# Four tiles of a SwiGLU layer from seven block products back to eight

## The chip, the cores and the metric

The kernel runs on one core of a Trainium2 chip. The metric is the device time of one execution in microseconds (us), from the first instruction to the last with the little that lies around them. The engines that matter here are TensorE (PE, matrix products), VectorE (DVE, element-wise work on two operands), ScalarE (ACT, element-wise functions and copies) and the DMA queue of SyncE (SP), which fetches all weights.

## What is computed

A decoder trunk of two layers over 512 tokens of width 1024, in float32. Each layer is an attention mixer, then a SwiGLU feed-forward block, each behind a norm whose scale and shift come from a vector `c`:

```
for l in range(2):
    sh1, sc1, g1, sh2, sc2, g2 = split(silu(c) @ ada_w[l] + ada_b[l], 6)
    h = rms_norm(x, norm_mix[l]) * (1 + sc1) + sh1
    y = mixer(h)                       # layer 0: two kinds of attention; layer 1: windowed
    x = x + g1 * (y @ w_out[l])
    h = rms_norm(x, norm_ffn[l]) * (1 + sc2) + sh2
    x = x + g2 * ((silu(h @ ffn_gate[l]) * (h @ ffn_up[l])) @ ffn_down[l])
```

The change lies in `h @ ffn_gate[0]` and `h @ ffn_up[0]`: 512 tokens by 1024 by 2816, twice.

## The kernel before

**Precision.** Every float32 product is made of three: an operand is split into a high part `hi` (rounded) and a low part `lo` (what is left), and `mm3` (L441) issues hi·hi, hi·lo and lo·hi into one accumulator. The split of an operand costs a copy on ACT (hi) and a subtraction on DVE (lo).

**Feed-forward block.** The 2816 hidden features are 22 tiles of 128, in two parts of 11 (`FPARTS`; tiles 0 to 10, then 11 to 21). After each part `reduce_out` (L1124) multiplies its hidden tiles by the down weights. A tile needs a 1024 by 128 block of the gate weights and one of the up weights, one DMA of 1 MB (`raw`), and its products are made in one of two ways:

- `ffn_tile` (L1153), eight block products: for each of 8 blocks of the inner dimension, gate and up, one `mm3` over all 512 tokens. That is 8 x 2 x 3 = 48 matmuls of 512 columns. The weights are split by `split_w` (L571): four subtractions of 128x512 on DVE. Two instructions of DVE take the result.
- `ffn_seven` (L1190), seven block products in place of eight, of the kind that Strassen's and Winograd's schemes use: the products run over half of the tokens (256 columns), 7 x 4 x 3 = 84 matmuls, on sums of weight blocks. `prep_seven` (L579) makes these sums and splits them: on DVE three instructions of 128x1024 and five of 128x512 per tile. Six instructions of DVE combine the products and split the hidden tile. The sums on the token side are made once per layer by `combos` (L1167): 24 instructions on DVE.

Before, tiles 0 to 2 of both layers went through `ffn_tile`, all others through `ffn_seven` (L569, L1240). Two of the first tiles are done in two halves of the tokens, since the norm ends by halves.

**Background work.** In layer 0's feed-forward block the modulation vectors that come later (the last of layer 0 and all six of layer 1) are computed in between by `mod_rest` (L693) as weighted sums on DVE: one step of two instructions on 128x512 after each tile (`NBG[0] = 1`), four steps after each output tile of `reduce_out`. Layer 1 has none of it. Its DMAs share the three `raw` buffers with the weights.

**Buffers.** Prepared weights lie in a pool `w` of 13 buffers of 128x1024: a tile in eight products holds 4, one in seven holds 7 and an eighth for a while. Accumulators (`ps`) are 8 banks.

**Order.** Operations are recorded first and put in order by `Sched` (L163 on): a list scheduler walks through them with the planner's own durations, gives DVE's operations due times worked back from PE's order, does this in up to eight rounds and keeps the round that it thinks shortest. So the place of each instruction on each engine is fixed when the kernel is built, buffers are handed out in that order, and each engine runs its own list strictly in order. A different list of operations in one place can change the order everywhere.

Of the kernel before, what the change touches and what calls it, by code (L numbers as in the profile page):

```python
# [25 lines left out]
BIG = 1e30  # L26
NW, NT2 = 13, 59

SEVEN, DIRECT = (0, 1), 3
NBG = (1, 4)  # L30
TOPK = 128
LAM_INIT = 0.2
# [340 lines left out]
class Kern:  # L373
# [192 lines left out]

    def seven(self, i):
        name, idx, _ = self.units[i]
        return name[:2] == "wg" and int(name[2]) in SEVEN and idx >= DIRECT  # L569

    def split_w(self, i, src, n, step, e="DVE"):  # L571
        hi, lo = (self.s.tile("w", "w", (P, 1024), FR)[:, :n] for _ in range(2))
# [194 lines left out]

    def norm_tile(self, l, n, k, c, r, H):
        sh = self.mod[l][:, 3 * n, k:k + 1]
        if n == 1 and l in SEVEN:  # L770
            if c.start == 0:
                if k == 0:
                    self.hf = []
                self.hf.append(self.t2("T"))
            t = self.hf[k][:, c]
        else:
            t = self.t2("nt")[:, c]
        hi, lo = H[k][0][:, c], H[k][1][:, c]
        self.stt(t, self.x[k][:, c], self.G[l][n][:, k:k + 1], r, OP.mult, OP.mult)
        self.act(hi, t, AF.Identity, bias=sh)  # L780
        self.stt(lo, t, sh, hi.bitcast(F), OP.add, OP.subtract)
# [443 lines left out]
    def ffn(self, l, H, last):  # L1225
        T = None
        for pi, (a, b) in enumerate(FPARTS):
            hid = [(self.t2("hid", dt=FR), self.t2("hid", dt=FR)) for _ in range(a, b)]
            W = {}

            def w(f):
                if f not in W:
                    W[f] = self.unit()
                return W[f]
            jobs = []
            if pi == 0:
                jobs = [(a + e, c) for c in HALVES for e in range(2)]
            jobs += [(f, ALL) for f in range(a + len(jobs) // 2, b)]
            for f, c in jobs:
                if l not in SEVEN or f < DIRECT:  # L1240
                    sg = self.ffn_tile(H, f, c, w(f), hid[f - a])
                else:
                    T = T or self.combos(l)
                    sg = self.ffn_seven(H, T, w(f), hid[f - a])
                self.lnexp = []
                if l == 0 and f == FT - 1:
                    self.act_table([sg])
                self.run_bg(NBG[0])
            self.reduce_out(l, hid, 5, pi == 1, last if pi == 1 else lambda m, c: None)
# [125 lines left out]
```

## Time and profile before

| | |
|---|---|
| time, median of 3 runs | 1195.58 us (1195.43 to 1197.99) |
| the profiled execution: its own time | 1197.88 us |
| the profiled execution: its span | 1196.1 us, granted TensorE clock 0.993 |
| busy: PE, DVE, ACT, POOL | 97%, 77%, 51%, 7% |
| layer 0's feed-forward block | about 301 to 674 us of the span |
| layer 1's feed-forward block | about 843 to 1196 us |

The page's busy share of PE is high all along, so the rows to look at are those that show where PE stands still, and what it waits for there. Matmuls overlap in the trace (one of 256 columns is recorded as 283 ns while a new one starts every 120 ns), so rates are read from counts over long windows and not from the mean of one.

### The profile page before, as it was taken

The page shows a single profiled execution, that of the slowest core. Times are in us where ns is not written, and L with a number is a line of the kernel's source. Part 1 is how long each engine was busy: PE and PEld are TensorE (multiplying, and loading weights), DVE is VectorE, ACT ScalarE, POOL GpSimd, SP SyncE. Part 2 cuts the span into 40 slices and gives each one's busy share as a digit, 9 for nine tenths or more (in the row PEclk, how much of TensorE's full clock was granted, in tenths as well). Part 3 has the DMA queues.
Part 4 walks back from the last instruction along what each step waited for, and adds up shares of the span by engine and source line. Part 5 has one row for each costly group of instructions (what it writes and reads, how often), then busy time and mean ns, then how long its engine had stood idle before and what let it go on. Part 6 is the DMA issues. An engine that isn't in the chain of part 4 may idle for free.

```text
span 1196.1 us, 20044 instructions
## 1 busy us (share of the span) xinstructions
PE 1163.8 (97%) x7792; PEld 1003.9 (84%) x7792; DVE 924.7 (77%) x2008; ACT 613.0 (51%) x1416; POOL 83.1 (7%) x224
## 2 busy tenths in 40 slices
PE   6989899999989999999999999999999999999998
PEld 3867677679989988999889976668999988999988
DVE  5589999856998978899984867755999844688831
ACT  5554266864754531354642657774766532566510
POOL 0132332300000000000000021100000000000000
PEclk9999999999998999999999999999999999999999
DMA  9635614012233377745372121012123342123411
GB/s 349 246 128 176 224 59 141 36 37 71 71 141 141 110 290 282 245 148 193 126 263 108 71 106 72 1 36 107 62 81 106 113 152 71 71 107 106 151 44 37
DMA packets 32432, 151.81 MB, mean 127 GB/s; under 512 B 3152, under 2 KB 4304, under 8 KB 21072
## 3 DMA queue, kind: packets, MB, share of 16 engines
q1 hardware_dynamic: 32336, 150.52, 35.3%
q8 instruction: 61, 1.00, 0.3%
q14 instruction: 35, 0.29, 0.1%
HBM read 148.41 MB, written 2.10 MB: 126 GB/s over the span
## 4 chain that ended last, share of the span: by engine, by line
PE 83%; DVE 8%; ACT 1%; issue 0%; DVEq 0%
PE ps L434 79%; PE ps L445 4%; DVE w L476 2%; DVE t L491 1%; DVE t L911 1%; DVE sm L910 1%; DVE t L476 1%; ACT t L460 1%; DVE raw L476 0%; DVE t L496 0%; ACT w L460 0%; DVE sm L502 0%; DVE t L484 0%; DVE x L491 0%; DVE ps L476 0%
## 5 line engine op out<-in xcount | busy, mean ns | idle before, releaser
L434 PE MATMUL ps<-t,w 128*128 128x256 f32 (+2 forms) x5664 | 822.9, 306 | 10.6 <-ACT t L460 5.7
L434 PEld LDWEIGHTS ps<-t,w 128*128 128x128 f32 x5664 | 759.6, 192 | 64.5 <-ACT t L460 9.2
L460 ACT ACTIVATE w<-raw 128x512 fp32r<-128x512 f32 (+1 forms) x364 | 227.7, 668 | 154.3 <-PE ps L434 98.8
L476 DVE TENSOR_TENSOR w<-raw,w 128x512 fp32r<-128x512 f32 (+1 forms) x340 | 249.7, 762 | 56.2 <-PE ps L434 42.7
L460 ACT ACTIVATE t<-ps 128x256 f32<-128x256 f32 (+6 forms) x388 | 154.6, 426 | 198.5 <-PE ps L434 131.7
L434 PE MATMUL ps<-w,t 128*128 128x512 f32 (+1 forms) x768 | 191.4, 391 | 0.8 <-DVE t L491 0.8
L434 PEld LDWEIGHTS ps<-w,t 128*128 128x128 f32 x768 | 133.1, 190 | 35.1 <-issue 8.2
L476 DVE TENSOR_TENSOR t<-t,t 128x256 f32<-128x256 f32 (+3 forms) x163 | 83.5, 536 | 15.8 <-ACT t L460 15.8
L476 DVE TENSOR_TENSOR t<-ps,t 128x256 f32<-128x256 f32 (+4 forms) x196 | 76.5, 410 | 20.1 <-ACT t L460 10.3
L491 DVE SCALAR_TENSOR_TENSOR x<-ps,mod,x 128x512 f32<-128x512 f32 (+1 forms) x64 | 39.3, 615 | 65.8 <-PE ps L434 65.6
L434 PE MATMUL ps<-t,t 64*128 64x256 f32 (+5 forms) x592 | 87.9, 357 | 0.7 <-ACT t L460 0.4
L434 PEld LDWEIGHTS ps<-t,t 64*128 64x128 f32 (+2 forms) x592 | 56.5, 186 | 32.9 <-issue 19.5
L491 DVE SCALAR_TENSOR_TENSOR t<-raw,cond,t 128x512 f32<-128x512 f32 x112 | 77.8, 746 | 1.4 <-DMA raw<-in_ada 1.4
L460 ACT ACTIVATE t<-t 128x512 fp32r<-128x512 f32 (+3 forms) x109 | 55.0, 522 | 32.5 <-DVE t L476 31.9
L460 ACT ACTIVATE t<-t,sm 128x256 f32<-128x256 f32 (+3 forms) x128 | 65.5, 515 | 11.9 <-DVE sm L496 11.1
L445 PE MATMUL ps<-cst,t 128*128 128x128 f32 x388 | 61.1, 278 | 8.9 <-DVE t L476 7.3
L445 PEld LDWEIGHTS ps<-cst,t 128*128 128x128 f32 x388 | 45.0, 140 | 29.4 <-DVE t L476 7.0
L460 ACT ACTIVATE w<-w 128x1024 fp32r<-128x1024 f32 x38 | 40.2, 1058 | 43.9 <-PE ps L434 41.5
L496 DVE CUSTOM_DVE_ANT_0 t<-ps,cst 128x256 f32<-128x256 f32 (+3 forms) x104 | 39.3, 409 | 26.1 <-PE ps L434 26.0
L476 DVE TENSOR_TENSOR w<-w 128x1024 fp32r<-128x1024 f32 x38 | 46.4, 1222 | 10.7 <-PE ps L434 10.4
L484 POOL TENSOR_SCALAR sm<-sm 128x8 f32<-128x8 f32 (+2 forms) x64 | 16.4, 256 | 514.6 <-DVE sm L502 502.3
L460 ACT ACTIVATE t<-t,mod 128x256 fp32r<-128x256 f32 (+2 forms) x72 | 37.8, 572 | 24.1 <-DVE t L491 24.0
(74 smaller groups left out, 620.4 us busy)
## 6 DMA issues: line engine op xcount, KB each, us to landing
raw<-in_wg SPq DMA_DIRECT2D x44, 1024.0 KB, 4.8
raw<-in_ada SPq DMA_DIRECT2D x40, 1024.0 KB, 5.3
raw<-in_wd SPq DMA_DIRECT2D x20, 1024.0 KB, 4.8
raw<-in_w0c SPq DMA_DIRECT2D x10, 1024.0 KB, 6.3
t<-in_ada SPq DMA_DIRECT2D x32, 256.0 KB, 6.6
raw<-in_wo SPq DMA_DIRECT2D x8, 1024.0 KB, 4.8
raw<-in_w1c SPq DMA_DIRECT2D x6, 1024.0 KB, 4.9
x<-in_x SPq DMA_DIRECT2D x8, 256.0 KB, 4.4
```

What stands on the lines that cost most here:

```text
L434: self.nc.tensor.matmul(o.ap(), l.ap(), r.ap(), start=st, stop=sp, skip_group_check=True)
L445: self.s.op("PE", 107, lambda: self.nc.tensor.transpose(out.ap(), src.ap(), self.ident.ap()), [out], [src, self.ident])
L460: self.nc.scalar.activation(out.ap(), src.ap(), func, **kw)
L476: lambda: self.eng(e).tensor_tensor(out.ap(), a.ap(), b.ap(), op=op), [out], [a, b])
L484: self.eng(e).tensor_scalar(out.ap(), a.ap(), val(s1), val(s2), op0=op0, **kw)
L491: lambda: self.eng(e).scalar_tensor_tensor(out.ap(), a.ap(), val(s), b.ap(), op0=op0, op1=op1),
L496: lambda: self.nc.vector.tensor_tensor_reduce(out.ap(), a.ap(), b.ap(), op0=OP.add, op1=OP.min, scale=scale, scalar=3e38, accum_out=accum. ...
L910: self.s.op("DVE", 65 + 1.05 * n, lambda m8=m8: self.nc.vector.max(m8.ap(), sc.ap()), [m8], [sc])
L911: self.s.op("DVE", 65 + 1.05 * n, lambda m8=m8: self.nc.vector.match_replace(sc.ap(), m8.ap(), sc.ap(), -3e38), [sc], [m8, sc])
```

## The change

Four tiles of layer 0 go back from `ffn_seven` to `ffn_tile`: tiles 4 and 6 (the fifth and seventh of the first part) and tiles 11 and 13 (the first and third of the second). `EIGHT` lists by layer which tiles use eight block products. Layer 1 keeps 0, 1 and 2. The line of `norm_tile` says the same as before, since both layers were in `SEVEN`.

```diff
-SEVEN, DIRECT = (0, 1), 3
+EIGHT = ((0, 1, 2, 4, 6, 11, 13), (0, 1, 2))
@@ def seven(self, i)
-        return name[:2] == "wg" and int(name[2]) in SEVEN and idx >= DIRECT
+        return name[:2] == "wg" and idx not in EIGHT[int(name[2])]
@@ def norm_tile(self, l, n, k, c, r, H)
-        if n == 1 and l in SEVEN:
+        if n == 1:
@@ def ffn(self, l, H, last)
-                if l not in SEVEN or f < DIRECT:
+                if f in EIGHT[l]:
                     sg = self.ffn_tile(H, f, c, w(f), hid[f - a])
```

The order is worked out anew. On PE it is the same up to the middle of layer 0's mixer and differs in places from there on; DVE's differs from a little earlier. Three places on DVE, the engine that prepares the weights.

DVE where tile 4's weights are prepared, from the first instruction of the modulation on (`t<-raw,cond`). `w<-raw,w` and `w<-w` are pieces of a tile's preparation, `<-ps` takes a product. Before:

```order
L484 TENSOR_SCALAR t_4149<-raw,cond 128x512
L484 TENSOR_SCALAR t_4159<-raw,cond 128x512
L491 SCALAR_TENSOR_TENSOR t_4149<-raw,cond,t_4149 128x512
L491 SCALAR_TENSOR_TENSOR t_4159<-raw,cond,t_4159 128x512
L476 TENSOR_TENSOR w<-w 128x1024
L476 TENSOR_TENSOR w<-raw,w 128x512 x2
L476 TENSOR_TENSOR t_4154<-ps,t_4133 128x256
L476 TENSOR_TENSOR w<-raw,w 128x512
```

Now:

```order
L476 TENSOR_TENSOR w<-raw,w 128x512 x6
L484 TENSOR_SCALAR t_4139<-raw,cond 128x512
L476 TENSOR_TENSOR ps<-ps,t_4122 128x256
L484 TENSOR_SCALAR t_4148<-raw,cond 128x512
L491 SCALAR_TENSOR_TENSOR t_4139<-raw,cond,t_4139 128x512
L491 SCALAR_TENSOR_TENSOR t_4148<-raw,cond,t_4148 128x512
```

Before, four of tile 4's pieces stood behind the modulation's first four instructions; now all four of its pieces (the last four of the `x6`; the first two are tile 3's) stand ahead of them.

DVE where tile 5's weights are prepared. Before:

```order
L476 TENSOR_TENSOR w<-raw 128x1024
L476 TENSOR_TENSOR w<-raw,w 128x1024
L476 TENSOR_TENSOR raw<-w,raw 128x512
L476 TENSOR_TENSOR w<-w 128x1024
L476 TENSOR_TENSOR w<-raw,w 128x512
L476 TENSOR_TENSOR raw<-raw 128x512
L476 TENSOR_TENSOR ps<-ps,t_4238 128x256
L491 SCALAR_TENSOR_TENSOR t_4149<-raw,cond,t_4149 128x512
L491 SCALAR_TENSOR_TENSOR t_4159<-raw,cond,t_4159 128x512
L476 TENSOR_TENSOR w<-raw 128x1024
L476 TENSOR_TENSOR w<-raw,w 128x512
L476 TENSOR_TENSOR raw<-w,raw 128x512
```

Now:

```order
L476 TENSOR_TENSOR w<-raw 128x1024
L476 TENSOR_TENSOR w<-raw,w 128x1024
L476 TENSOR_TENSOR raw<-w,raw 128x512
L476 TENSOR_TENSOR w<-w 128x1024
L476 TENSOR_TENSOR w<-raw,w 128x512
L476 TENSOR_TENSOR raw<-raw 128x512
L491 SCALAR_TENSOR_TENSOR t_4139<-raw,cond,t_4139 128x512
L491 SCALAR_TENSOR_TENSOR t_4148<-raw,cond,t_4148 128x512
L476 TENSOR_TENSOR w<-raw,w 128x512
L491 SCALAR_TENSOR_TENSOR t_4139<-raw,cond,t_4139 128x512
L491 SCALAR_TENSOR_TENSOR t_4148<-raw,cond,t_4148 128x512
L476 TENSOR_TENSOR w<-raw,w 128x512
```

Before, tile 6's preparation (the second `w<-raw 128x1024`) began ahead of the last pieces of tile 5; now tile 5 is finished with nothing of tile 6 ahead of it.

DVE at the end of the preparation of tile 17, in the second part. Before:

```order
L476 TENSOR_TENSOR w<-raw,w 128x1024
L476 TENSOR_TENSOR raw<-w,raw 128x512
L476 TENSOR_TENSOR t_6335<-ps,t_6285 128x256
L476 TENSOR_TENSOR raw<-raw 128x512
L476 TENSOR_TENSOR w<-w 128x1024
L491 SCALAR_TENSOR_TENSOR t_6062<-raw,cond,t_6062 128x512
L476 TENSOR_TENSOR w<-raw,w 128x512 x2
L491 SCALAR_TENSOR_TENSOR t_6069<-raw,cond,t_6069 128x512
L476 TENSOR_TENSOR ps<-ps,t_6425 128x256
L491 SCALAR_TENSOR_TENSOR t_6062<-raw,cond,t_6062 128x512
L491 SCALAR_TENSOR_TENSOR t_6069<-raw,cond,t_6069 128x512
L476 TENSOR_TENSOR w<-raw,w 128x512 x2
```

Now:

```order
L476 TENSOR_TENSOR w<-raw,w 128x1024
L476 TENSOR_TENSOR w<-raw 128x1024
L476 TENSOR_TENSOR w<-raw,w 128x512
L476 TENSOR_TENSOR ps<-ps,t_6122 128x256
L476 TENSOR_TENSOR raw<-w,raw 128x512
L476 TENSOR_TENSOR w<-raw,w 128x512
L476 TENSOR_TENSOR raw<-raw 128x512
L476 TENSOR_TENSOR t_6071<-ps,t_6041 128x256
L476 TENSOR_TENSOR w<-raw 128x1024
L491 SCALAR_TENSOR_TENSOR t_5786<-raw,cond,t_5786 128x512
L476 TENSOR_TENSOR t_6149<-ps,t_6122 128x256
L476 TENSOR_TENSOR w<-w 128x1024
```

Before, the last piece of tile 17 (the first of the closing `x2`) stood behind seven of the eight pieces of tile 18 and four modulation instructions; now two pieces of tile 18 and one modulation instruction stand among those of tile 17, and its last two pieces follow right behind the rows shown.

## Rows read from the trace of the kernel before

**Rows 1.** The page's part 2: busy tenths in 40 slices.
```profile
PE   6989899999989999999999999999999999999998
DVE  5589999856998978899984867755999844688831
```

**Rows 2.** Windows: stretch, length; PE, PEld, DVE, ACT, POOL busy; PEclk; DMA.
```profile
346.00:368.00 22.00, 17.26 (x112) 16.09 (x112) 19.38 (x33) 11.40 (x22) 0.00 (x0) 0.84 0.53 194
549.00:585.00 36.00, 31.66 (x254) 29.74 (x253) 35.77 (x60) 20.04 (x39) 0.00 (x0) 1.00 0.43 157
```

**Rows 3.** Timeline of PE, 346 to 368 us; in brackets idle time before, releaser.
```profile
345.81 1.48 PE L434 MATMUL ps<-t,w 128*128 128x256 f32 x11
347.77 4.69 PE L434 MATMUL ps<-t,w 128*128 128x256 f32 x36 [0.47 <-ACT t L460]
352.93 1.69 PE L434 MATMUL ps<-t,w 128*128 128x256 f32 x12 [0.47 <-ACT t L460]
355.64 1.69 PE L434 MATMUL ps<-t,w 128*128 128x256 f32 x12 [1.02 <-ACT t L460]
359.38 2.07 PE L434 MATMUL ps<-t,w 128*128 128x256 f32 x12 [2.04 <-DVE t L476]
362.18 5.99 PE L434 MATMUL ps<-t,w 128*128 128x256 f32 x29 [0.73 <-DVE t L476]
```

**Rows 4.** Timeline of PE, 549 to 585 us.
```profile
551.63 6.02 PE L434 MATMUL ps<-t,w 128*128 128x256 f32 x48 [1.01 <-ACT t L460]
558.12 3.13 PE L434 MATMUL ps<-t,w 128*128 128x256 f32 x24 [0.47 <-ACT t L460]
561.90 7.46 PE L434 MATMUL ps<-t,w 128*128 128x256 f32 x60 [0.66 <-DVE t L476]
570.78 4.58 PE L434 MATMUL ps<-t,w 128*128 128x256 f32 x36 [1.42 <-ACT t L460]
...
579.50 3.13 PE L434 MATMUL ps<-t,w 128*128 128x256 f32 x24 [0.31 <-DVE t L476]
583.11 1.69 PE L434 MATMUL ps<-t,w 128*128 128x256 f32 x12 [0.47 <-ACT t L460]
```

**Rows 5.** Chain of waits in 346 to 368 us, then 549 to 585: shares.
```profile
by line: PE ps L434 32.7%; DVE w L476 27.2%; ACT w L460 11.5%; DVE t L491 9.9%; DVE raw L476 7.6%; issue 3.4%; DVE t L476 3.1%; ACT t L460 3.0%; DVE ps L476 2.0%
...
by line: PE ps L434 34.2%; DVE w L476 32.7%; DVE t L491 13.3%; DVE raw L476 8.4%; issue 5.7%; DVE t L476 3.1%; ACT t L460 1.1%; DVE ps L476 0.9%; PE ps L445 0.6%; DVEq L476 0.1%
```

**Rows 6.** Windows: the clock behind the longest wait.
```profile
362.00:366.00 4.00, 3.83 (x18) 3.83 (x19) 3.38 (x10) 2.41 (x8) 0.00 (x0) 0.50 0.96 380
```

**Rows 7.** Windows in layer 1: tiles in seven products, then down products.
```profile
885.00:945.00 60.00, 60.00 (x502) 60.00 (x501) 54.57 (x90) 38.63 (x73) 0.00 (x0) 1.00 0.31 107
970.00:1015.00 45.00, 45.00 (x200) 37.26 (x199) 18.02 (x24) 9.83 (x14) 0.00 (x0) 1.00 0.27 94
```

**Rows 8.** Groups by form on DVE: count, busy us, mean ns, idle before.
```profile
L476 DVE TENSOR_TENSOR w<-raw,w 128x512 fp32r<-128x512 f32 x300 | 203.1, 706 | 43.4 <-PE ps L434 30.1 <-issue 7.4 <-ACT w L460 5.4
L491 DVE SCALAR_TENSOR_TENSOR t<-raw,cond,t 128x512 f32<-128x512 f32 x112 | 77.8, 746 | 1.4 <-DMA raw<-in_ada 1.4
L476 DVE TENSOR_TENSOR t<-ps,t 128x256 f32<-128x256 f32 x122 | 49.6, 419 | 6.8 <-PE ps L434 6.0 <-ACT w L460 0.7
L476 DVE TENSOR_TENSOR w<-raw,w 128x1024 fp32r<-128x1024 f32 x38 | 46.5, 1223 | 12.8 <-PE ps L434 12.6
...
L476 DVE TENSOR_TENSOR t<-t,t 128x512 fp32r<-128x512 f32 x56 | 37.4, 686 | 4.1 <-ACT t L460 4.1
```

**Rows 9.** Timeline of DVE, 339 to 362 us.
```profile
339.53 0.87 DVE L484 TENSOR_SCALAR t<-raw,cond 128x512 f32<-128x512 f32 x2
...
344.91 2.73 DVE L491 SCALAR_TENSOR_TENSOR t<-raw,cond,t 128x512 f32<-128x512 f32 x4
```

**Rows 10.** Windows in the mixers of layer 0 and layer 1.
```profile
160.00:300.00 140.00, 139.54 (x852) 106.20 (x851) 106.46 (x324) 89.45 (x261) 30.31 (x78) 1.00 0.20 68
674.00:845.00 171.00, 168.63 (x980) 126.48 (x979) 117.34 (x391) 106.57 (x325) 19.66 (x76) 1.00 0.17 62
```

## The prediction

> **What bounds the kernel now.** The slices come first [rows 1]: PE is busy nearly everywhere, so the kernel is bound by PE, and a change can gain only where PE stands still or runs slowly, or by giving PE less to do. This one gives PE more to do, so it must gain in waits. The slices of layer 0's feed-forward block show two dips of PE beside DVE digits of 9, near 350 us and near 560 us. The windows of the two stretches [rows 2] say the same in numbers: DVE is busy 19.38 of 22 us and 35.77 of 36, PE has holes. Next is the rate without holes [rows 7]: 502 matmuls of 256 columns in 60 us are one per 0.120 us, 200 of 512 columns in 45 us one per 0.227 us (up to three of each count lie over the window's edge, so the distances could be 0.1195 and 0.225).
>
> *The first hole.* At 0.120 us the 22 us from 346 on would count about 185 matmuls; there are 112 [rows 2]. 73 x 0.120 = 8.8 us are lost. The timeline [rows 3] has them piece by piece: five waits with 0.47 + 0.47 + 1.02 + 2.04 + 0.73 = 4.7 us idle; then the last two rows, 41 matmuls in 8.1 us where 4.9 would do, 3.1 us, because the granted clock falls to 0.50 behind the longest waits [rows 6], its lower level of 1.2 GHz; the rest, about 0.9 us, is the restart after five waits. Between 7.8 (what is seen piece by piece) and 8.8 I take 8.6.
>
> *The second hole.* Six waits, 1.01 + 0.47 + 0.66 + 1.42 + 0.31 + 0.47 = 4.3 us idle [rows 4]. By the count, 36 us would hold 302 matmuls and hold 254 [rows 2]: 5.8 us. The clock stays at 1.00. I take 5.2. Together 13.8 us are there to be won, 12.1 to 14.6.
>
> *Who makes PE wait.* Seven of the eleven waits end with ACT [rows 3, 4], but the chain through each stretch [rows 5] spends 50% and 58% of the time on DVE's lines and 14.5% and 1% on ACT's: ACT waits for DVE in turn. DVE's lines there are `w` and `raw` (preparing weights for seven products) and `t` L491 (the modulation).
>
> **Why DVE falls behind.** In layer 1, where the same tiles run without background work, DVE is busy 54.57 of 60 us [rows 7], in which PE does 60 / (84 x 0.120 = 10.08) = 5.95 tiles: 9.2 us of DVE per tile in seven products, against 10.08 of PE. A step of the modulation adds two instructions: four in a row take 2.73 us where one takes 0.746 [rows 8, 9], so each costs 0.66 and the step 1.3. That makes 10.5 us of DVE for 10.08 of PE: a debt of 0.4 us with every tile. In the first part `combos` adds 24 instructions, 16 of 0.42 and 8 of 0.69 us [rows 8], 12 us, just ahead of the first hole. A tile in eight products needs on DVE four pieces of 0.706 and two instructions of 0.69 (the row of 0.686; the other that takes a product of 512 columns is bounded by it): 4.2 us, while PE takes longer over it. Each tile that changes back takes 5 us off DVE, the four 20 us.
>
> **The change part by part.** *PE.* Four tiles lose 84 matmuls of 256 columns and get 48 of 512: 48 x 0.227 - 84 x 0.120 = 10.90 - 10.08 = 0.82 us each, 3.3 us in all (2.9 to 3.4 by the two readings of the rates). All of it lies on PE, which sets the end, so it is paid in full.
>
> The page "TensorE: Matmul & The Clock Gate" of the Trainium skill, section "Back-to-back issue gap", would price this higher: N / 2.4 + 2.5 ns, 215.8 and 109.2 ns, which as an estimate gives 10.36 - 9.17 = 1.19 us a tile, 4.7 us in all, and 1187.0 us as the result. The trace differs: it has 0.011 us more than the rule for a matmul of either width, and seven products have more matmuls that pay it; the sum goes by the trace.
>
> *Tile 4 and 5, the first hole.* The last 96 matmuls ahead of 347.1 us (the end of the first run [rows 3]) are tile 3's 84 and 12 of tile 4's, so tile 3 began at 335.6 us. Changed, PE is through with tile 3 at 345.7 and with tile 4 at 356.6. DVE began the modulation at 339.53 [rows 9]; ahead of it stood four pieces of tile 4 (two of 1.22, two of 0.69, 3.8 us), which become four of 0.706 (2.8 us), so tile 4 is ready at about 338.5, 7 us ahead of PE. From there to tile 5's last piece DVE now has 25 instructions: 12 of the modulation (9.0 us by mean durations), 5 that take products (2.4) and tile 5's eight (3 x 1.22 + 2 x 0.69 + 3 x 0.706 = 7.15): 18.5 us, or 16.4 with 0.085 of overlap each [rows 8, 9]. Tile 5 is ready between 354.9 and 357.0, its first pieces some 7 us before that; PE wants the first at 356.6 and the last, six products later, at 365. The hole goes, and with it the slow clock.
>
> *Tile 6* has the same relief before tile 7. Its second pair of buffers comes free only when tile 4 ends, for which DVE then stands in line for a moment, with 10 us of tile 5 as cover.
>
> *Tiles 11 and 13, the second hole.* Counted from the first instruction that takes a product of tile 12 to tile 17's last piece, DVE has 86 instructions before: the preparation of 13 to 17 (35.8 us), 8 pieces of the next and the last (7.2), 16 of the modulation (11.9), 22 around the products (10.5): 65.4 us, 58 with the overlap taken off. PE takes 7.2 for the rest of tile 12 and 4 x 10.08 to tile 17, 47.5 us, and wants the last piece at 56: late. Changed there are 65 instructions: 14 to 17 (28.6), two pieces of tile 18 (1.9), 10 of the modulation (7.5), 21 around the products (9.9), 47.9 or 42.5 us; PE takes 7.2 + 10.9 + 3 x 10.08 = 48.3. DVE is 6 us early, and the tiles after that can eat 0.4 us each of it, 1.6 to tile 21. This hole goes too.
>
> *What hides what.* ACT loses work as well; nobody waits for it then. The DMA queue moves the same bytes. The buffers `w` fill sooner (before, DVE stood 30.1 and 12.6 us in line for PE ahead of two kinds of pieces [rows 8]); a DVE that is ahead stands there longer, and an instruction that takes a product can be queued behind it. That is the price if the cover is gone: one wait of 0.5 to 1 us, as in [rows 4], for each such place.
>
> *What else moves.* The order changes in both mixers. PE idles there 0.5 us and 2.4 us [rows 10], so at most 2 us could be won; what can be lost has no row, the nearest are single waits of 0.5 to 2.0 us [rows 3, 4], and three or four of them make 4 us. Between -2 and +4 I take +0.5, since in the new order most moved instructions stand a few places from where they stood.
>
> **The sum.** -13.8 + 3.3 + 0.5 = -10.0 us. On the profiled execution: span 1196.1 to 1186.1, its own time 1197.9 to 1187.9. That execution is 2.3 us over the median, so from the median of 1195.6 the forecast is **1185.6 us**. The ends are -14.6 + 2.9 - 2 = -13.7 (1181.9) and -12.1 + 3.4 + 4 = -4.7 (1190.9).
>
> **The rivals.** *One hole only.* If DVE's debt comes back between tiles 14 and 21 (eight tiles in a row with the modulation beside them), the second hole stays: 1195.6 - 8.6 + 3.3 = 1190.3; if tile 5 is late after all, the first: 1195.6 - 5.2 + 3.3 = 1193.7. For it: the debt of 0.4 us a tile is still there. Against it: the 6 us in hand.
>
> *Slower: it is ACT's list that PE waits for.* Seven of eleven waits end with ACT, whose list is strictly in order; if the copies of weights ahead of the copies that take products are what is late, an eight-product tile changes nothing about it, the holes stay, and 3.3 us are paid: 1198.9 us. It decides from the point where less than 3.3 of the 13.8 us goes. Against it: ACT is busy 11.40 of 22 us there [rows 2] and has 14.5% of the chain and 1% [rows 5].
>
> *The new order costs elsewhere* more than I allow, 4 us or so, in a mixer: 1189 to 1190. For it: nothing in the trace of before shows the new neighbours. Against it: most of what moved, moved by a few places.
>
> That the change does not do what it says is ruled out by the new order: the four tiles' matmuls have 512 columns and their preparation four pieces.
>
> **How the numbers follow.** Both holes go: 0.69. One goes: 0.15 (0.11 the first alone, 0.04 the second alone). New order costs: 0.08. ACT: 0.08. The range goes from the forecast's lower end, 1182, over the first hole alone and the costs elsewhere to 1192, and leaves out the second hole alone, ACT and some tail, about 0.15. A measurement of this kernel can tell 0.2% from no change, 2.4 us: faster means below 1193.2. Faster: 0.69 + 0.08 + 0.11 = 0.88; the same: 0.04, the second hole alone; slower: 0.08.
>
> **What would show it.** In the changed profile PE's timeline should have no wait over 0.3 us between tiles 4 and 7 and between 14 and 21, the granted clock should stay at 1.00 around 360 us, and DVE's total should fall by some 20 us. Matmuls of 256 columns: 336 fewer; of 512: 192 more, one per 0.227 us. It would be wrong if waits for ACT stay where they were, if a wait shows up behind DVE's queueing for `w`, or if either mixer is longer than before by more than 1 us.

## The result, and the profile after

The changed kernel takes **1183.16 us** (median; 1183.09 to 1184.63) beside 1195.85 us for the kernel before (1195.43 to 1197.99): a ratio of 0.9893, 95% interval 0.9876 to 0.9910. That is 12.7 us less, where 10.0 were forecast; the time lies in the range, 1.2 us above its lower end. The profiled execution has a span of 1181.3 us at a granted clock of 0.996, against 1196.1 at 0.993.

The slices of the changed kernel, to be set beside [rows 1]:

```profile
PE   6989999999999999999999999999999999999998
DVE  6589999846998889889984866756999843788831
```

PE's dip near 350 us (the twelfth slice) is a 9 now, and so is the fifth, in layer 0's mixer. The hole near 560 us had no digit of its own there: it shows in windows only. Nearly the same tiles as in [rows 2], now 3 and 14 us earlier (in the second stretch the end of tile 16, then 17 to 19, where [rows 2] had 17 to 19), and the time around which the clock had fallen [rows 6]; columns are stretch, length, busy time and count of PE, PEld, DVE, ACT and POOL, then the granted clock:

```profile
343.00:365.00 22.00, 22.00 (x139) 19.72 (x137) 20.71 (x34) 11.39 (x20) 0.00 (x0) 1.00 0.53 192
535.00:571.00 36.00, 36.00 (x305) 35.45 (x304) 32.93 (x51) 20.43 (x39) 0.00 (x0) 1.00 0.45 160
360.00:366.00 6.00, 6.00 (x47) 5.01 (x47) 5.79 (x9) 3.62 (x6) 0.00 (x0) 1.00 0.21 57
```

In the second stretch all matmuls have 256 columns in both kernels, so the counts can be compared: 305 where there were 254. The timelines of PE there have no idle time at all, and its list of waits is empty for the whole block; a row ends where the form of the matmul changes, and brackets with a wait, as in [rows 3, 4], are missing:

```profile
337.77 27.34 PE L434 MATMUL ps<-t,w 128*128 128x256 f32 x178
365.03 0.64 PE L434 MATMUL ps<-t,ones 128*32 128x256 f32 x8
...
498.50 64.84 PE L434 MATMUL ps<-t,w 128*128 128x256 f32 x498
```

The `ones` row is the modulation's own matmul on PE: at the end of each vector it sums what DVE has accumulated. It will matter below.

**Where the time went.** Both kernels have two rows that mark the ends of layer 0's feed-forward block: the matmuls with `ones` of 128 by 128 for the second half of the tokens, ahead of that block and ahead of layer 1's mixer. PE's timeline before, then after:

```profile
304.50 0.59 PE L434 MATMUL ps<-t,ones 128*128 128x256 f32 x2
...
673.73 0.59 PE L434 MATMUL ps<-t,ones 128*128 128x256 f32 x2
```

```profile
301.37 0.59 PE L434 MATMUL ps<-t,ones 128*128 128x256 f32 x2
...
659.16 0.59 PE L434 MATMUL ps<-t,ones 128*128 128x256 f32 x2
```

Up to the first row the changed kernel is 3.1 us shorter (304.50 to 301.37), between them 11.4 us (369.23 to 357.79), and from there to the end of the span 0.2 us (522.4 to 522.1). So 3.1 of the 14.8 us by which the spans differ lie ahead of the block, where no instruction was changed, only their order. They are not all the order's. PE's list is the same in all kernels here up to its 947th matmul, in the middle of layer 0's mixer. The rows in which the lists part (the first three matmuls of each are the same) start at, before and after:

```profile
170.13 2.34 PE L434 MATMUL ps<-w,t 128*128 128x512 f32 x9
```

```profile
169.11 0.96 PE L434 MATMUL ps<-w,t 128*128 128x512 f32 x3
```

So 1.0 us of the 3.1 lies ahead of these rows, in a list that is the same, and from them to the first mark it is 2.1 us (134.37 to 132.26). In the other runs below these rows start anywhere from 168.70 to 170.86 us, whatever the order, so the 1.0 is within what executions differ by.

### The profile page after: what moved, and what is told of

Its sections match the earlier page's. It is cut to its first block, busy times and chain, and to the rows that moved or that the text cites. A ratio compares the mean times of both kernels' runs of the same rounds, so it can differ in the third digit from the quotient of the medians.

```text
span 1181.3 us, 19707 instructions
## 1 busy us (share of the span) xinstructions
PE 1158.7 (98%) x7648; PEld 995.8 (84%) x7648; DVE 903.3 (76%) x1976; ACT 604.6 (51%) x1396; POOL 85.3 (7%) x224
## 4 chain that ended last, share of the span: by engine, by line
PE 86%; DVE 5%; ACT 1%; POOL 0%; issue 0%
PE ps L434 82%; PE ps L445 3%; DVE t L911 1%; DVE t L491 1%; DVE sm L910 1%; DVE w L476 1%; ACT t L460 0%; DVE t L476 0%; POOL sm L476 0%; DVE t L496 0%; DVE sm L502 0%; DVE t L484 0%; ACT sm L460 0%; POOL sm L484 0%; DVE sm L491 0%
## 5 line engine op out<-in xcount | busy, mean ns | idle before, releaser
L434 PEld LDWEIGHTS ps<-t,w 128*128 128x128 f32 x5520 | 751.9, 191 | 57.5 <-issue 6.2
L460 ACT ACTIVATE w<-raw 128x512 fp32r<-128x512 f32 (+1 forms) x364 | 225.3, 663 | 160.7 <-PE ps L434 92.6
L476 DVE TENSOR_TENSOR w<-raw,w 128x512 fp32r<-128x512 f32 (+1 forms) x340 | 244.6, 749 | 58.0 <-PE ps L434 43.0
L460 ACT ACTIVATE t<-ps 128x256 f32<-128x256 f32 (+6 forms) x376 | 151.0, 430 | 206.6 <-PE ps L434 145.7
L476 DVE TENSOR_TENSOR t<-ps,t 128x256 f32<-128x256 f32 (+4 forms) x188 | 73.7, 415 | 23.1 <-ACT t L460 12.2
L491 DVE SCALAR_TENSOR_TENSOR x<-ps,mod,x 128x512 f32<-128x512 f32 (+1 forms) x64 | 39.4, 615 | 66.2 <-PE ps L434 65.9
L491 DVE SCALAR_TENSOR_TENSOR t<-raw,cond,t 128x512 f32<-128x512 f32 x112 | 77.8, 746 | 0.0
L460 ACT ACTIVATE w<-w 128x1024 fp32r<-128x1024 f32 x34 | 36.1, 1060 | 32.6 <-PE ps L434 25.2
L484 POOL TENSOR_SCALAR sm<-sm 128x8 f32<-128x8 f32 (+2 forms) x64 | 16.7, 261 | 476.7 <-DVE sm L502 456.8
L476 DVE TENSOR_TENSOR w<-w 128x1024 fp32r<-128x1024 f32 x34 | 41.5, 1220 | 10.9 <-PE ps L434 10.8
L476 DVE TENSOR_TENSOR w<-raw 128x1024 f32<-128x1024 f32 x34 | 41.5, 1221 | 10.1 <-PE ps L434 9.8
```

The source lines that it names most:

```text
L434: self.nc.tensor.matmul(o.ap(), l.ap(), r.ap(), start=st, stop=sp, skip_group_check=True)
L460: self.nc.scalar.activation(out.ap(), src.ap(), func, **kw)
L476: lambda: self.eng(e).tensor_tensor(out.ap(), a.ap(), b.ap(), op=op), [out], [a, b])
L484: self.eng(e).tensor_scalar(out.ap(), a.ap(), val(s1), val(s2), op0=op0, **kw)
L491: lambda: self.eng(e).scalar_tensor_tensor(out.ap(), a.ap(), val(s), b.ap(), op0=op0, op1=op1),
```

## The experiments

Up to eight orders are worked out for a kernel and one is kept. The kernel before kept number 1, the changed one and all runs below but the second number 3, and that alone sets PE's order in layer 0's mixer: it is the same in all that kept the same number. The first two runs take tiles and order apart.

**Tiles of before, order number 3.**

```diff
         for r in range(8):
 ...
-            if best is None or self.length < best[0]:
+            if r == 3:
```

> The kernel before with all its tiles as they were; only the order is another: the planner's fourth round is kept (numbered 3, the one the changed kernel got) in place of its second (numbered 1). Up to the first feed-forward tiles the lists of all engines are then those of the changed kernel. Theory (the mixer of layer 0 is 3.1 us shorter in the changed kernel because of the order alone): tile 2 of layer 0 begins near 321.6 us in place of 324.7, both holes stay in some form, the time is about 1192.8. Rival A (the 3.1 us have to do with the four tiles or with chance): tile 2 begins near 324.7, the time is 1195.9. Rival B (the order closes the holes too, the eight-product tiles were not needed): about 1180 to 1184.

Measured: 1199.24 us, ratio 1.0027 [1.0016, 1.0038]: slower than before. The first mark comes 3.5 us earlier (300.96), 2.1 of it by the order, but the block between the marks takes 374.46 us where it took 369.23. The theory's 1192.8 fails. It forgot that a hole does not end earlier when PE comes earlier, since DVE sets its end: tile 7 began at 383.8 us, before at 382.7. The marks, then PE's waits over 0.5 us in the block, in this kernel's timeline:

```profile
300.96 0.59 PE L434 MATMUL ps<-t,ones 128*128 128x256 f32 x2
...
675.42 0.59 PE L434 MATMUL ps<-t,ones 128*128 128x256 f32 x2
```

```profile
369.33 1.64 PE L434 MATMUL ps<-t,ones 128*32 128x256 f32 x8 [5.60 <-DVE t L491]
...
528.11 4.43 PE L434 MATMUL ps<-t,w 128*128 128x256 f32 x24 [2.05 <-ACT t L460]
536.46 40.97 PE L434 MATMUL ps<-t,w 128*128 128x256 f32 x327 [3.92 <-DVE t L476]
```

and the window behind the first of them:

```profile
368.00:374.00 6.00, 4.19 (x20) 2.96 (x21) 6.00 (x14) 2.29 (x5) 0.00 (x0) 0.50 0.74 291
```

The debt now comes out in one piece: PE stands 5.60 us in front of the modulation's own `ones` matmul, whose last input (L491) DVE has not written yet, while tile 6, the next in PE's list, had its last piece written at 365.5. DVE reached those instructions only at 367.11, behind preparations of tile 7 (its timeline, from the first of them on):

```profile
363.03 1.22 DVE L476 TENSOR_TENSOR w<-raw 128x1024 f32<-128x1024 f32 x1
...
367.11 2.73 DVE L491 SCALAR_TENSOR_TENSOR t<-raw,cond,t 128x512 f32<-128x512 f32 x4
```

The window shows the clock at 0.50 around the end of that wait and behind it. So the modulation hurts in two ways, by DVE's time and by a matmul in PE's strictly ordered list.

**Tiles of after, order number 1** (`if r == 1:` in the same place of the changed kernel).

> The changed kernel, four tiles in eight products, with the order of the planner's second round (numbered 1, the one the kernel before had); up to the first feed-forward tiles the lists of all engines are those of the kernel before. Theory (order and tiles are separate): tile 2 of layer 0 begins near 324.7 us, no hole at 346 to 368 nor at 549 to 585 us, the time is 1183.2 + 3.1 = 1186.3. Rival A (the 3.1 us go with the tiles): 1183.2. Rival B (the gain is the order's): about 1192 to 1196, with holes.

Measured: 1186.95 us, ratio 0.9918 [0.9905, 0.9930]. First mark at 304.06, as before within 0.44 us (134.35 us behind the row in which the lists part, before 134.37); the block takes 359.02 us, 10.2 less than before. The marks, then PE's waits between 330 and 660 us (engine, what was waited for: total, times, longest):

```profile
304.06 0.59 PE L434 MATMUL ps<-t,ones 128*128 128x256 f32 x2
...
663.08 0.59 PE L434 MATMUL ps<-t,ones 128*128 128x256 f32 x2
```

```profile
PE ps L434 <- ACT t L460: 0.7, 1, 0.7
```

With the order's part held still the tiles are worth 10.2 us between the marks; what is over in the changed kernel is the order's, 3.8 us by the medians and 3.0 by the two ratios.

**One pair at a time**, both in order number 3, so the kernel to compare with is the first run (374.46 us between the marks).

```diff
-EIGHT = ((0, 1, 2, 4, 6, 11, 13), (0, 1, 2))
+EIGHT = ((0, 1, 2, 4, 6), (0, 1, 2))
```

> Only tiles 4 and 6 in eight products; 11 and 13 stay in seven. The order in the mixer is that of the changed kernel. Theory (two separate holes, each closed by its own pair): the first hole goes, worth 8.6, the pair costs PE 1.6, the second hole stays with 5.2, order -3.1: 1195.9 - 8.6 + 1.6 - 3.1 = 1185.8, with PE waits of 4 us together between 545 and 580 us. Rival A (the second hole is the tail of the debt that the first part leaves behind): the second hole shrinks as well, about 1181 to 1182, since 1.6 us of PE time is saved against the changed kernel. Rival B (tile 4 and 6 do nothing, 11 and 13 do it all): about 1194.

Measured: 1188.79 us, ratio 0.9936 [0.9924, 0.9948]; between the marks 363.67, 10.8 less. The first hole is gone, the second stays: four waits between 520 and 533 us, a fifth at 575, 5.8 us in all. PE's waits between 325 and 660 us:

```profile
PE ps L434 <- ACT t L460: 3.8, 4, 1.2
PE ps L434 <- DVE t L476: 2.1, 1, 2.1
```

```diff
-EIGHT = ((0, 1, 2, 4, 6, 11, 13), (0, 1, 2))
+EIGHT = ((0, 1, 2, 11, 13), (0, 1, 2))
```

> Only tiles 11 and 13 in eight products; 4 and 6 stay in seven. The order in the mixer is that of the changed kernel. Theory (two separate holes): the second hole goes, worth 5.2, the pair costs PE 1.6, the first hole stays with 8.6 and its stretch at half the clock, order -3.1: 1195.9 - 5.2 + 1.6 - 3.1 = 1189.2. Rival A (the new order alone narrows the first hole): below 1186. Rival B (the debt moves on and opens the second hole all the same): about 1194.

Measured: 1191.88 us, ratio 0.9958 [0.9944, 0.9972]; between the marks 366.97, 7.5 less. The second hole is gone and the wait of 5.60 us for L491 is there again, 0.43 us later. So each pair closes its own hole and leaves the other alone; no rival holds. Both times came out some 3 us above the theory's, since it took the holes' sizes from order number 1. The parts add up to 18.3 us where both pairs together bring 16.7 (374.46 to 357.79), so they are not quite independent.

**What a tile costs PE.** The changed kernel with the same four tiles in layer 1 as well.

```diff
-EIGHT = ((0, 1, 2, 4, 6, 11, 13), (0, 1, 2))
+EIGHT = ((0, 1, 2, 4, 6, 11, 13), (0, 1, 2, 4, 6, 11, 13))
```

> The changed kernel, and in layer 1 the same four tiles (4, 6, 11, 13) in eight products as well. Layer 1 has no modulation and DVE keeps ahead of PE there, so nothing is to be won: this measures what a tile costs PE. Theory (0.82 us a tile, from the distances of 0.120 and 0.227 us): +3.3 us, 1186.5. Rival A (distances N / 2.4 plus 2.5 ns, as the Trainium skill's page on the matmul and the clock gate has them): +4.7 us, 1187.9. Rival B (the extra slack of DVE buys something in layer 1 too): no more than +1 us, 1184.

Measured: 1186.29 us, ratio 0.9914 [0.9899, 0.9928]. Between the marks 357.79, to the hundredth as in the changed kernel; from the second mark to the end 525.4 in place of 522.1. The four tiles cost 3.3 us, which is the theory's 0.82 each, and buy nothing where DVE is not late. By the rule on the page "TensorE: Matmul & The Clock Gate" of the Trainium skill (section "Back-to-back issue gap"), which the section gives for an isolated matmul, the estimate was 4.7 us; this run differs from it. The marks of this run:

```profile
302.26 0.59 PE L434 MATMUL ps<-t,ones 128*128 128x256 f32 x2
...
660.05 0.59 PE L434 MATMUL ps<-t,ones 128*128 128x256 f32 x2
```

**The modulation taken from the tiles in seven products**, with the tiles of before (order number 3).

```diff
-                self.run_bg(NBG[0])
+                self.run_bg(2 if f < 3 else 0)
```

> The tiles of the kernel before (only 0 to 2 in eight products), but the modulation is taken away from the tiles in seven: two steps after each of tiles 0 to 2 (ten steps in all, for the vector of layer 0), none after tiles 3 to 21, the rest in both runs of the down products. The planner keeps the same round as in the changed kernel, so the kernel to set beside it is the one before in that order (1199.2 us). Theory (the debt is the modulation's 1.3 us of DVE a tile): the second hole goes altogether, the first goes or leaves no more than 2 us, since the sums on the token side still stand there; between tile 2 and tile 21 PE saves 18 to 21 us against that kernel, with no price: about 1179 to 1181. Rival A (the preparation of the weights and the sums on the token side alone make DVE late): holes stay, above 1190. Rival B (the steps come back as a debt in the down products, where four of them already stand after each output tile): 1185 to 1190, with waits between 430 and 480 us or 600 and 670 us.

Measured: 1190.40 us, ratio 0.9952 [0.9936, 0.9967]; between the marks 367.09, 7.4 less than the 374.46, not 18 to 21. The second hole shrinks to two waits of 0.40 and 1.22 us, so there the modulation was the cause. The first one moved to tile 3:

```profile
335.51 3.13 PE L434 MATMUL ps<-t,w 128*128 128x256 f32 x24 [0.47 <-ACT t L460]
341.57 2.93 PE L434 MATMUL ps<-t,w 128*128 128x256 f32 x12 [2.94 <-ACT t L460]
345.47 1.73 PE L434 MATMUL ps<-t,ones 128*32 128x256 f32 x8 [0.96 <-DVE t L491]
```

Ten steps, 13 us of DVE by the prediction's 1.3 each, were put beside the 12 us of `combos`, all ahead of tile 4. The theory fails here. The reading that fits is that the first hole is the heap of work between the norm and tile 4, and that a load moved earlier onto that heap only moves the hole; no run took the modulation off the first part altogether, so what `combos` alone would cost PE is not shown.

**The second pair replaced by moving the modulation.** Tiles 4 and 6 in eight products, 11 and 13 in seven, no modulation after the tiles of the second part (its 18 steps go to the second run of the down products).

```diff
-EIGHT = ((0, 1, 2, 4, 6, 11, 13), (0, 1, 2))
-NBG = (1, 4)
+EIGHT = ((0, 1, 2, 4, 6), (0, 1, 2))
+NBG = ((1, 0), 4)
 ...
-                self.run_bg(NBG[0])
+                self.run_bg(NBG[0][pi])
```

> Tiles 4 and 6 in eight products as in the change; 11 and 13 stay in seven, and in their place the modulation is kept away from the second part's tiles (those steps go to the second run of the down products). Theory (tiles 11 and 13 did nothing but take DVE's debt away, and cost PE 0.82 us each): no second hole, 1183.2 - 1.6 = 1181.5. Rival A (the debt is made by the preparation itself): the second hole of about 9 us as with tiles 4 and 6 alone, 1188.8. Rival B (the moved steps are late for the second layer's norm, or make the down products wait): 1184 or more, with waits between 600 and 680 us.

Measured: 1183.76 us, ratio 0.9893 [0.9877, 0.9908]; between the marks 357.85, the same as the changed kernel's 357.79. The hole is down to waits of 0.94 and 0.21 us at 519 and 525 us; the whole list of PE's waits between 325 and 655 us:

```profile
PE ps L434 <- ACT t L460: 0.9, 1, 0.9
PE ps L434 <- DVE t L476: 0.2, 1, 0.2
```

PE saves the 1.6 us for two tiles and loses as much in what is left of the hole, so the result is a tie where 1.6 us less was expected; DVE is a little late in the second part without the modulation too.

**Tile 4 alone**: as the run before, with `EIGHT = ((0, 1, 2, 4), (0, 1, 2))`.

> As the run with the modulation kept away from the second part's tiles, but of the first part tile 4 alone is in eight products; tile 6 goes back to seven. Theory (the first hole is the sums on the token side, 12 us, and two or three steps of modulation; tile 4 gives 5 us back and the hole is 11 us in this order): part of the hole stays, 3 to 6 us, now nearer to tile 7: about 1184 to 1187. Rival A (one tile is enough): 0.8 us less than the run with both. Rival B (tile 6 does most): 1190 or more.

Measured: 1184.52 us, ratio 0.9901 [0.9886, 0.9915]; between the marks 358.81, 1.0 more than with both. Two waits in tile 7, 0.47 and 1.30 us, so less was left than the theory's 3 to 6: tile 4 does most of the work for the first hole, and tile 6 pays for itself by a fraction of a microsecond at best.

**The sums on the token side on GpSimd** (tiles of before, order number 3).

```diff
-            self.tt(p[:, c1], f[:, c1], f[:, c2], OP.subtract)
+            self.tt(p[:, c1], f[:, c1], f[:, c2], OP.subtract, e="POOL" if l == 0 else "DVE")
 ...
```

> The tiles of the kernel before; in layer 0 the 16 sums on the token side (128x256, 0.42 us each on DVE) run on GpSimd. The planner keeps the round of the changed kernel, so the kernel to set beside it is the one before in that order (1199.2 us, a first hole of 11 us of which PE stands 5.6 in one wait for the modulation's last instruction). Theory (the first hole is DVE's debt, so what is taken off DVE ahead of it comes off the hole): 16 x 0.42 = 6.7 us off the first hole, which leaves about 4.5; the second hole is untouched; about 1192.5. Rival A (GpSimd, at an estimated 0.7 us a sum from the row of 1.43 us for twice the columns, with four sums in a chain, is late itself): tile 3 waits for the sums, 1196 or more. Rival B (the hole has nothing to do with the sums, only with the modulation): 1198 to 1199.

Measured: 1200.17 us, ratio 1.0033 [1.0022, 1.0043]; between the marks 374.20, no better than 374.46. GpSimd takes 1.17 to 1.19 us a sum in the mean, not 0.7 (the shortest took 0.77), and tile 3 waits as rival A says. But DVE gained nothing by it either. The window in which GpSimd works, in this kernel, then the same stretch in the first run (fifth pair of numbers GpSimd):

```profile
315.00:329.00 14.00, 14.00 (x89) 12.69 (x88) 14.00 (x12) 7.23 (x13) 13.44 (x12) 1.00 0.21 75
```

```profile
315.00:329.00 14.00, 14.00 (x88) 12.65 (x88) 13.51 (x25) 10.02 (x17) 0.00 (x0) 1.00 0.21 75
```

DVE does 12 instructions in place of 25, one for each of GpSimd's. One form of them, 309 to 330 us, again with and then without GpSimd at work (last numbers: busy us, mean ns):

```profile
L476 DVE TENSOR_TENSOR t<-t,t 128x512 fp32r<-128x512 f32 x2 | 2.4, 1227 | 0.0
```

```profile
L476 DVE TENSOR_TENSOR t<-t,t 128x512 fp32r<-128x512 f32 x8 | 5.1, 685 | 0.0
```

An instruction of DVE takes 0.54 us longer, so 16 sums on GpSimd, at one for one, cost DVE an estimated 8.6 us and took 6.7 off it. The page "SBUF — State Buffer" of the Trainium skill, section "SBUF: two separate sides", says that a DVE operation with two inputs in SBUF and a GpSimd operation lock one pair of ports for a whole instruction and the other one waits; one for one, as here, is what that would look like.

**The same with tile 4** (as the tile-4 run, sums of layer 0 on GpSimd).

> As the run with tile 4 alone and no modulation beside the second part's tiles (1184.5 us), with the 16 sums of layer 0 on GpSimd as well. Theory: the 2.2 us of waits before tile 7 that were left go, nothing else moves: 1182.3. Rival A (GpSimd late for tile 3): 1185 or more. Rival B (those waits are due to tile 6's own preparation): 1184.5.

Measured: 1189.01 us, ratio 0.9932 [0.9914, 0.9951]; rival A, with waits of 0.50 and 3.18 us at tile 3 (340 to 345 us).

**A third tile for the second part**: as the run with the second pair replaced, with tile 13 in eight products, `EIGHT = ((0, 1, 2, 4, 6, 13), (0, 1, 2))`.

> As the run with tiles 4 and 6 in eight products and no modulation beside the second part's tiles (1183.8 us), with tile 13 in eight products as well. Theory (that run's 1.9 us of waits between tiles 13 and 15 are a small debt, and one tile's 5 us cover it): -1.5 to -1.9 for the waits, +0.8 for PE: 1182.7 to 1183.1. Rival A (waits stay, the tile only costs): 1184.6. Rival B (the waits move to tile 16 or later): 1184.

Measured: 1182.46 us, ratio 0.9887 [0.9870, 0.9904]; between the marks 357.19, 0.6 less than in the changed kernel, and no wait of PE in the block. It is the lowest time here, but its runs (1181.22 to 1185.39) overlap those of the changed kernel; 0.7 us is less than this measurement can tell.

**A known load put back.** The changed kernel with two steps of the modulation after each tile of the second part.

```diff
-NBG = (1, 4)
+NBG = ((1, 2), 4)
 ...
-                self.run_bg(NBG[0])
+                self.run_bg(NBG[0][pi])
```

> The changed kernel with two steps of the modulation in place of one after each tile of the second part, until there are none left (18 steps, so after tiles 11 to 19). This puts a known load back on DVE. Theory (seven products take DVE 9.2 us a tile, a step 1.3 us, and at tile 17 the changed kernel has 6 us in hand): ten more instructions of the modulation by tile 17 are 6.6 us, which just uses up the 6 us; tiles 18 to 20 then owe 1.7 us each, so PE waits 3 to 5 us in all between tiles 17 and 21: 1186 to 1188. Rival A (DVE has much more in hand than that): no waits, 1183. Rival B (the hold is smaller, or a wait behind the queue for buffers sets in): 8 us or more of waits, from tile 14 or 15 on, 1191 and more.

Measured: 1193.12 us, ratio 0.9975 [0.9965, 0.9986]; between the marks 367.64, 9.9 more than the changed kernel. The waits:

```profile
545.05 1.69 PE L434 MATMUL ps<-t,w 128*128 128x256 f32 x12 [0.64 <-ACT t L460]
547.22 1.69 PE L434 MATMUL ps<-t,w 128*128 128x256 f32 x12 [0.47 <-ACT t L460]
549.91 23.29 PE L434 MATMUL ps<-t,w 128*128 128x256 f32 x192 [1.01 <-ACT t L460]
577.67 1.73 PE L434 MATMUL ps<-t,ones 128*32 128x256 f32 x8 [4.47 <-DVE t L491]
583.67 1.70 PE L434 MATMUL ps<-t,w 128*128 128x256 f32 x12 [0.42 <-DVE t L476]
```

They begin at tile 17, where the theory's 6 us run out, and end at tile 19, but come to 7.0 us, where 3 to 5 were expected, with slow clock and restarts behind them: the place is the theory's, the time is rival B's (1191 and more). The biggest is again PE in front of the modulation's own matmul: a place that the count of pieces against tiles leaves out.

## Why the prediction was right, step by step

**The holes and the price.** Forecast -13.8 + 3.3 = -10.5 us. With the planner's round held still, the second run measured -10.2 between the marks, so the sum of the sizes read from [rows 2 to 4] was right for that order; no run has the two holes apart in it, and in order number 3 the same tiles bring 16.7. The price of 3.3 us, from distances of 0.120 and 0.227 us [rows 7], was measured as 3.3 in layer 1. Two counts in the working are slightly high: at 0.120 us, 22 and 36 us hold 183 and 300 matmuls, not 185 and 302, which takes 0.3 us off the upper figure of each hole.

**Who makes PE wait.** Seven of eleven waits ended with ACT [rows 3, 4], and the prediction held by the chain [rows 5] that DVE was behind them. All waits for ACT are gone, with ACT as busy as it was in the two stretches (11.39 us for 11.40, 20.43 for 20.04). That alone does not rule ACT out, since the four tiles change its list too. The runs with the modulation moved or doubled do, in the second part: a step is two instructions of DVE, and without the steps the waits there shrink from 5.8 to 1.2 us with tiles 11 and 13 still in seven products, while with twice as many, three of the five waits that come back end with ACT. So there DVE is late, and ACT waits for it in turn. In the first part the evidence for DVE is the wait of 5.60 us, in the first and the fourth run, that ended with DVE itself. That it is the modulation on top of `combos` is argued from the sums: taking the modulation from the later tiles did not close that hole, tile 4 did, and no run separates the two.

**Tiles 4 and 5.** DVE's timeline of the changed kernel: tile 4's four pieces are the last of the first row, tile 5's first and last piece the next two.

```profile
330.51 3.78 DVE L476 TENSOR_TENSOR w<-raw,w 128x512 fp32r<-128x512 f32 x6
...
342.29 1.22 DVE L476 TENSOR_TENSOR w<-raw 128x1024 f32<-128x1024 f32 x1
...
350.75 0.69 DVE L476 TENSOR_TENSOR w<-raw,w 128x512 fp32r<-128x512 f32 x1
```

Tile 4 was ready at 334.3, 6.8 us ahead of its first matmul (341.1; forecast 7). Tile 5 was ready at 351.4, 17.1 us after tile 4 (forecast 16.4 to 18.5), and PE came for it at 353.5. **Tile 17** was ready at 542.4. From the first instruction that takes a product of tile 12 (493.6) to there are 65 instructions, as forecast, in 48.8 us, of which DVE is busy 42.8 (forecast 42.5) and stands the other 6.0, nearly all of it waiting for PE: the 6 us in hand are there. The last pieces are wanted late in a tile (tile 17 began at 540.5, its last product at 550.9), which the forecast's comparison with the tile's start left out. DVE's total fell from 924.7 to 903.3 us, 21.4 (forecast 20).

**The step that was mis-sized** is "order elsewhere": +0.5 us, between -2 and +4. It measured -2.1 in layer 0's mixer, just outside that bound, and nothing behind the block (522.1 us in both orders); inside the block the order brought another -1.2 (359.02 against 357.79), for which the forecast had no term. Together that is -3.3 by the traces (3.0 by the ratios, 3.8 by the medians), and it is why the time came out near the lower end of the range. The bound of -2 rested on PE's idle time in the windows of the mixers [rows 10], 0.5 us in 140. That reading was wrong: a busy PE is not a PE at one rate. The window of the changed kernel that answers to the first of [rows 10]:

```profile
157.00:297.00 140.00, 139.58 (x863) 106.80 (x862) 107.54 (x330) 90.97 (x263) 31.74 (x78) 1.00 0.20 68
```

PE is as busy as before, 139.58 to 139.54 us, and does 863 matmuls in place of 852. Cleaner than counts in a window is the stretch from the row in which the lists part to the first mark, which holds the same matmuls in another order: 134.37 and 134.35 us in the two kernels with order number 1, 132.18 to 132.26 in the twelve with number 3. A part of the 2.1 us can be read from the traces: a matmul of 64 rows behind one of 128, or the other way round, starts about 0.1 us later than the median distance of its own form (0.326 us for 0.231 in the commonest), and there are 62 such changes in this stretch before and 56 after, 0.6 us. What makes the rest was not settled; no single form of matmul has the larger part of it.

**The other bounds** held: no wait behind DVE's queue for `w`, and everything behind the second mark, layer 1's mixer in it, is 0.2 us shorter. That order and tiles do not simply add was not foreseen: order number 3 is 3 us worse than number 1 with the old tiles, and 3.8 us better with the new ones.

**Why 14.8 us by the spans is 12.7 by the medians.** The profiled execution of the kernel before took 1197.88 us, 2.0 over that kernel's median; that of the changed kernel lies at its median. The times of the kernel before, 1194.3 to 1200.2 in all sessions, go with the granted clock at the ends: 1194.3 to 1197.1 where it is 0.996 or more, 1198.9 to 1200.2 where it is 0.991. The profiled execution, at 0.993, has a slow stretch behind the first hole [rows 6].

## What to carry over

A bound for "the order changes elsewhere" must not be read from idle time alone: compare the time between the same two instructions, since two executions of one list can differ by 2 us (the start of the same row ranged over 2.2 us here), and where a planner chooses among several orders, look first whether the choice itself has changed. Holes that a second engine's debt makes end when that engine is done, so bringing the waiting engine there sooner gains nothing until the debt is paid. And a background job costs not only its engine's time: if its result is consumed by an instruction in the bound engine's list, everything behind that instruction waits for it.

## What the runs showed of the hardware

While GpSimd ran sums of 128x256 in SBUF, the instructions of DVE took about 0.54 us longer (one form 1227 ns for 685) and the two engines did one instruction each in turn, 12 and 12 in 14 us: work moved from DVE to GpSimd was no relief. And the granted clock stood at 0.50 in the window of 6 us around the end of PE's single wait of 5.60 us and behind it, as it had behind the shorter waits of [rows 6], so a hole costs more than its idle time. That the scatter of a kernel's times comes from such holes is not shown: the kernel before, with holes, scattered over 5.9 us, and the changed one over 1.5 in four runs, but a kernel without a wait in the block, the one with a third tile, over 4.2 in five.
